# A hybrid encoder step on one core: the order planner is given longer instruction times

## The chip, the cores and the metric

The kernel runs on one core of one Trainium2 chip. The metric is device microseconds (us) of one execution; lower is better.

## The reference

One inference step of a streaming encoder layer (depth 1, width 1024) for 2048 prompt tokens with 16 learned meta tokens in front, and for 64 tokens of a running stream with 512 cached keys. Of each stream:

```
hn   = rms_norm(x, norm_mix_g)
proj = hn @ w_in                       # columns split among three head groups
o    = concat[ diff_attention(...),    # 4 heads, two softmaxes each, p0 - lam * p1, block-causal by chunks of 64
               rg_lru(...),            # causal conv of 4, gates, linear recurrence over the tokens
               gla(...) ]              # gated linear attention, 4 heads, blocks of 64
x    = x + o @ w_out
hn   = rms_norm(x, norm_ffn_g)
x    = x + (gelu(causal_dwconv3(hn @ w_up)) * (hn @ w_gate)) @ w_down
y    = rms_norm(x, norm_final_g)
```

Outputs are y of both streams, the new keys and values, and the final states of the recurrences and the convolutions.

## The kernel before

**Precision and tiles.** All 2128 tokens lie side by side as columns. Each factor of a large product is split into a high part and a rest, and each product is three passes on TensorE (high by high, high by rest, rest by high), in a `k` loop over 8 slices of 128 rows. `w_split` loads a weight tile `raw` in its first use, splits it into `whi` (ScalarE) and `wlo` (Pool or VectorE), and parks both in DRAM (`WS`), from where later uses reload them.

**Three streams.** `dense()` first runs `win()` (the combined projection, six token blocks, PSUM tile `ps_w`, L645 and L647), then `ffn_group(g)` for three groups of tokens (512; 512; 336 + 256 + 512): `wout` (L1437), `up_gate` (tiles `pu` and `pg`, L1302) and `down` (tile `pd`, L1369, added into `x` by VectorE at L1375). `attention()` runs over 9 token chunks by 4 heads. A unit's scores (L1056, L1063 into `ps_sc`, of which there are two buffers) are followed by a minimum on VectorE (L1065, `NB`), an exponential on ScalarE (L1066, `pc`) and, when a row's factors `fr` are known, a mix on Pool and VectorE (L157, L1104); then come transposes (L1155, `ps_pt`), their split on ScalarE and VectorE (`ph`, `pl`) and the product with V (L1170, `ps_o`). The last step of a unit is `oo`, stored to `OT`. `recurrent()` runs the RG-LRU and the GLA chunk by chunk (products L726, L895 and others into `ps_r`; a chain of VectorE, ScalarE and Pool steps such as L890 and L899 between them).

**Who sets the order.** `Flow.run` interleaves the three streams in program order by rough step costs written into the kernel. While attention issues, its priority number is lowered by 30000, and while the recurrences issue by 16000, so that these go ahead of dense work wherever they can. The orders on the engines are fixed at build time by a planner, which is switched on where the program is built:

```
    with tile.TileContext(nc, schedule_with_timeline_sim=True) as tc:
        tile_hymba_step(tc, *args)
```

It plays the program through with an assumed duration for each instruction. Each engine takes, of the instructions whose inputs and buffers are free at that moment of the play, the one with the lowest priority number. The orders of this play are final: on the chip each engine goes through its list and waits in front of any instruction whose inputs are late, with everything behind it on that engine waiting too. The same holds for SyncE, which issues nearly all transfers.

**Borders.** Group 1 of the FFN (tokens 512 to 1024) needs attention and recurrences of chunks 0 to 4; the last group needs all of them, since it reads `OT` and takes over their memory (`mstack.close()`, then `open3()`).

## Time and profile before

| | |
|---|---|
| median of 3 runs | 2975.56 us (2971.42 to 2979.68) |
| profiled execution, its own time | 2973.88 us |
| its span | 2972.1 us, 44691 instructions |
| TensorE busy | 2845.5 us, 96% |
| VectorE, ScalarE, Pool busy | 1868.5, 1084.9 and 765.9 us (63%, 37%, 26%) |
| mean granted TensorE clock | 0.98 of full |

The span is the stretch from the first to the last instruction of the profiled execution; 1.8 us of its time lie around it. A share of busy time is a mean over stages with different loads; the stages are told apart by windows below. Full speed of the granted clock is 2.4 GHz, and the lower level is 1.2 GHz.

### The profile page before, as it was taken

To read this page: it belongs to the slowest core of one execution; us is meant where nothing else is said; L and a number is where in the kernel's file an instruction comes from. 1 tells how busy PE (TensorE), PEld (TensorE's weight loads), DVE (VectorE), ACT (ScalarE), POOL (GpSimd) and SP (SyncE) were. 2 spreads that over 40 slices of the span, in tenths; PEclk is the share of its full clock that TensorE was granted. 3 is DMA by queue.
4 is the path that set the end of the run, shared out by engine and by line. 5 is a ranking of instruction groups with operands and counts; after the bars stand their busy time and mean duration, and the time that the engine had idled before them with its cause. 6 is when DMAs were issued, how large, how long until landed. Compare 5 with 4: busy or idle time off the path is not lost.

```text
span 2972.1 us, 44691 instructions
## 1 busy us (share of the span) xinstructions
PE 2845.5 (96%) x16031; PEld 2504.7 (84%) x16031; DVE 1868.5 (63%) x3757; ACT 1084.9 (37%) x2526; POOL 765.9 (26%) x1171
## 2 busy tenths in 40 slices
PE   6999999999999999999999999999999999999998
PEld 5988999999877777877777888888989999989997
DVE  6467674658688899899888764444454333333335
ACT  5354533454455554555553432112231121212122
POOL 4224231323244454445433210000120000000001
PEclk9999999999999999999999999999999999999998
DMA  9987776687995887878775655955222222222222
GB/s 327 325 282 208 244 245 217 218 265 227 286 332 185 283 252 241 273 251 265 242 263 180 216 186 194 336 196 189 82 86 86 86 86 86 86 86 86 85 85 105
DMA packets 293628, 592.31 MB, mean 199 GB/s; under 512 B 32758, under 2 KB 171774, under 8 KB 293406
## 3 DMA queue, kind: packets, MB, share of 16 engines
q1 hardware_dynamic: 293262, 589.44, 59.7%
q8 instruction: 127, 2.08, 0.3%
q14 instruction: 95, 0.78, 0.1%
q10 hardware_dynamic: 144, 0.01, 0.0%
HBM read 414.40 MB, written 174.96 MB: 198 GB/s over the span
## 4 chain that ended last, share of the span: by engine, by line
PE 50%; DVE 8%; DMA 2%; issue 1%; POOL 1%; ACT 1%; SPq 0%; POOLq 0%; ACTq 0%; DVEq 0%
PE pd L1369 15%; PE pu L1302 14%; PE pg L1302 13%; PE pd L1437 4%; DVE pc L1104 2%; PE ps_o L1170 1%; DVE NB L1065 1%; PE ps_pt L1155 1%; DVE BD L890 1%; PE ps_sc L1063 1%; DVE y L439 1%; PE ps_sc L1056 1%; DVE cc L1326 0%; DVE x L1375 0%; DVE pl L160 0%
## 5 line engine op out<-in xcount | busy, mean ns | idle before, releaser
L1326 DVE SCALAR_TENSOR_TENSOR cc<-uh,prm,cc 128x512 f32<-128x512 f32 (+4 forms) x264 | 164.0, 628 | 268.2 <-ACT cc L1324 264.8
L1066 ACT ACTIVATE pc<-ps_sc,NB 128x512 f32<-128x512 f32 (+6 forms) x400 | 224.7, 563 | 287.0 <-DVE NB L1065 243.4
L1375 DVE TENSOR_TENSOR x<-x,pd 128x512 f32<-128x512 f32 (+2 forms) x320 | 195.7, 617 | 199.4 <-PE pd L1369 198.3
L1302 PE MATMUL pu<-h2h,whi 128*128 128x512 f32 (+2 forms) x880 | 315.7, 359 | 3.1 <-ACT h2h L154 2.6
L1369 PE MATMUL pd<-gh,whi 128*128 128x512 f32 (+2 forms) x880 | 314.9, 359 | 3.9 <-DVE x L1375 2.3
L1302 PE MATMUL pg<-h2h,whi 128*128 128x512 f32 (+2 forms) x880 | 315.7, 359 | 2.0 <-DMA whi<-WS 2.0
L1302 PE MATMUL pu<-h2l,whi 128*128 128x512 f32 (+2 forms) x880 | 315.4, 359 | 0.4 <-DVE h2l L160 0.4
L1302 PE MATMUL pu<-h2h,wlo 128*128 128x512 f32 (+2 forms) x880 | 315.7, 359 | 0.0
L1302 PE MATMUL pg<-h2h,wlo 128*128 128x512 f32 (+2 forms) x880 | 315.7, 359 | 0.0
L1302 PE MATMUL pg<-h2l,whi 128*128 128x512 f32 (+2 forms) x880 | 314.5, 357 | 0.0
L1369 PE MATMUL pd<-gh,wlo 128*128 128x512 f32 (+2 forms) x880 | 312.9, 356 | 0.0
L1369 PE MATMUL pd<-gl,whi 128*128 128x512 f32 (+2 forms) x880 | 312.7, 356 | 0.0
L1319 ACT ACTIVATE uh<-pu 128x336 f32<-128x336 f32 (+3 forms) x132 | 59.3, 465 | 587.7 <-PE pu L1302 585.8
L645 PE MATMUL ps_w<-hh,whi 128*128 128x384 f32 (+2 forms) x768 | 260.2, 341 | 14.2 <-ACT whi L154 10.5
L645 PE MATMUL ps_w<-hh,wlo 128*128 128x384 f32 (+2 forms) x768 | 259.7, 338 | 12.0 <-DVE wlo L160 5.0
L1065 DVE TENSOR_REDUCE NB<-ps_sc 128x1 f32<-128x512 f32 (+6 forms) x400 | 209.5, 530 | 96.1 <-PE ps_sc L1063 94.5
L645 PE MATMUL ps_w<-hl,whi 128*128 128x384 f32 (+2 forms) x768 | 258.3, 337 | 0.1
L261 POOL TENSOR_TENSOR wlo<-raw,whi 128x1024 fp32r<-128x1024 f32 (+2 forms) x63 | 153.4, 2434 | 165.2 <-ACT whi L154 145.8
L157 POOL TENSOR_SCALAR gh<-cc 128x336 fp32r<-128x336 f32 (+3 forms) x132 | 69.6, 530 | 477.2 <-DVE cc L1339 375.6
L157 POOL TENSOR_SCALAR pc<-pc,fr 128x512 f32<-128x512 f32 (+4 forms) x200 | 167.1, 855 | 97.8 <-DVE fr L1086 88.9
L1369 PEld LDWEIGHTS pd<-gh,whi 128*128 128x128 f32 x880 | 165.7, 188 | 26.9 <-DVE x L1375 4.0
L1302 PEld LDWEIGHTS pu<-h2h,whi 128*128 128x128 f32 x880 | 167.0, 190 | 24.8 <-ACT h2h L154 2.8
(331 smaller groups left out, 6981.2 us busy)
## 6 DMA issues: line engine op xcount, KB each, us to landing
whi<-WS SPq DMA_DIRECT2D x202, 512.0 KB, 4.4
wlo<-WS SPq DMA_DIRECT2D x202, 512.0 KB, 5.0
WS<-whi SPq DMA_DIRECT2D x94, 512.0 KB, 4.3
WS<-wlo SPq DMA_DIRECT2D x94, 512.0 KB, 6.4
Kc<-KHL SPq DMA_DIRECT2D x48, 512.0 KB, 5.4
V<-VHL SPq DMA_DIRECT2D x48, 512.0 KB, 5.0
Q<-QHL SPq DMA_DIRECT2D x64, 256.0 KB, 5.1
raw<-in_wu SPq DMA_DIRECT2D x22, 512.0 KB, 4.2
```

Source lines behind the costliest of these rows:

```text
L157: nc.gpsimd.tensor_scalar(out, in_, s, 1.0, ALU.mult, ALU.mult)
L261: nc.gpsimd.tensor_tensor(out=lo[:, :n], in0=t[:, :n], in1=f(hi[:, :n]), op=ALU.subtract)
L645: nc.tensor.matmul(ps[:, :n], lhsT=wx, rhs=hx, start=st_, stop=sp_)
L1065: nc.vector.tensor_reduce(NB[:qw, ti, m, ci:ci + 1], ps[:qw, :kt_], AX.X, ALU.min)
L1066: nc.scalar.activation(out=pv_[m][:qw, :kt_], in_=ps[:qw, :kt_], func=AF.Exp, scale=-1.0, bias=NB[:qw, ti, m, ci:ci + 1], accum_out=SS[:qw ...
L1104: nc.vector.scalar_tensor_tensor(out=p0, in0=p0, scalar=u.R[:qw, ti, 0, ci:ci + 1], in1=p1, op0=ALU.mult, op1=ALU.add)
L1302: nc.tensor.matmul(ps[:, :n], lhsT=w_[wi_][:, k * P:(k + 1) * P], rhs=hx, start=(k == 0 and i3 == 0), stop=(k == KT - 1 and i3 == 2))
L1319: nc.scalar.activation(out=uh[:, 2:2 + m], in_=pu[:, a:b], func=AF.Copy)
L1326: nc.vector.scalar_tensor_tensor(out=cc[:, :m], in0=uh[:, w:w + m], scalar=cw[w], in1=cc[:, :m], op0=ALU.mult, op1=ALU.add)
L1369: nc.tensor.matmul(ps[:, :n], lhsT=w_, rhs=g_[:, o:o + n], start=(j == 0 and i3 == 0), stop=(j == len(gts) - 1 and i3 == 2))
L1375: nc.vector.tensor_tensor(x2[b, ct], x2[b, ct], ps[:, :n], ALU.add)
L1437: nc.tensor.matmul(ps[:, :n], lhsT=w_, rhs=g_, start=(k == 0 and i3 == 0), stop=(k == KT - 1 and i3 == 2))
```

## The change

Only the planner's assumptions are changed, at the head of the file, before anything is built. No instruction is added, removed or altered. The table `CYCLE_T` holds the planner's cycle time of each engine's data path: VectorE's is multiplied by 1.4, ScalarE's by 1.15 and Pool's by 1.2. `PE_FULL_CLOCK_PASS_GAP_NS` is the time that the planner puts behind each matmul at the full clock, over the streaming of its columns; it is set to 13 ns. Times of transfers, of semaphores and of weight loads stay as they are.

```diff
 import concourse.tile as tile
 from concourse import mybir
 from concourse._compat import with_exitstack
+from concourse.hw_specs import TRN2Spec
 from concourse.masks import make_identity
+
+
+TRN2Spec.CYCLE_T = {
+    mybir.EngineType.DVE: 1.4 * TRN2Spec.CYCLE_T[mybir.EngineType.DVE],
+    mybir.EngineType.Activation: 1.15 * TRN2Spec.CYCLE_T[mybir.EngineType.Activation],
+    mybir.EngineType.Pool: 1.2 * TRN2Spec.CYCLE_T[mybir.EngineType.Pool],
+}
+TRN2Spec.PE_FULL_CLOCK_PASS_GAP_NS = 13.0
```

## Rows read from the trace of the kernel before

**Rows 1.** The windows view, whole engines; columns: window, length, busy (instructions), PEclk, DMA share, GB/s.
```profile
0.00:1800.00 1800.00, 1693.24 (x9559) 1477.93 (x9560) 1381.27 (x2900) 848.74 (x2101) 654.93 (x876) 0.97 0.77 250
...
0.00:50.00 50.00, 33.24 (x168) 30.03 (x168) 34.41 (x84) 24.56 (x49) 21.76 (x32) 0.93 0.91 322
50.00:100.00 50.00, 36.74 (x202) 34.90 (x203) 23.75 (x40) 22.06 (x40) 23.40 (x17) 0.86 0.97 334
...
1800.00:2000.00 200.00, 200.00 (x903) 165.82 (x902) 87.39 (x129) 35.74 (x56) 15.72 (x54) 1.00 0.70 249
2400.00:2700.00 300.00, 300.00 (x1797) 273.58 (x1796) 110.70 (x202) 55.59 (x102) 21.84 (x77) 1.00 0.24 85
```

**Rows 2.** Windows of 50 us with the lowest granted clock.
```profile
200.00:250.00 50.00, 42.43 (x256) 38.14 (x255) 37.98 (x107) 20.90 (x72) 17.44 (x33) 0.90 0.80 253
800.00:850.00 50.00, 40.81 (x206) 31.91 (x205) 42.66 (x84) 29.90 (x73) 22.82 (x28) 0.83 1.00 327
900.00:950.00 50.00, 45.37 (x211) 37.06 (x210) 46.63 (x92) 22.32 (x54) 21.63 (x22) 0.90 0.54 165
1600.00:1650.00 50.00, 44.56 (x197) 34.89 (x196) 47.50 (x101) 23.14 (x57) 23.53 (x26) 0.86 0.40 128
```

**Rows 3.** Waits of TensorE, whole run: total us, times, longest us.
```profile
PE ps_sc L1056 <- ACT pc L1066: 15.5, 16, 2.6
PE ps_sc L1056 <- DMA Q<-QHL: 7.9, 6, 1.9
PE ps_r L895 <- DVE att L899: 5.3, 6, 2.0
PE ps_o L1170 <- DVE pl L160: 4.7, 5, 1.6
PE ps_w L645 <- DMA wlo<-WS: 3.9, 2, 2.9
```

**Rows 4.** TensorE's timeline behind one such wait: start us, us, engine, line, instruction.
```profile
1010.09 0.50 PE L1056 MATMUL ps_sc<-Kc,Q 128*128 128x512 f32 x1 [2.25 <-ACT pc L1066]
...
1012.89 0.63 PE L1369 MATMUL pd<-gh,whi 128*128 128x512 f32 x1
1013.32 0.63 PE L1369 MATMUL pd<-gh,wlo 128*128 128x512 f32 x1
```

**Rows 5.** The chain that ended last, two dense products: start us, us, passes.
```profile
1877.63 5.44 PE pu L1302 x24
...
2455.67 5.60 PE pu L1302 x24
```

**Rows 6.** Groups by line and shape, VectorE and ScalarE: busy us, mean ns, idle before.
```profile
L1065 DVE TENSOR_REDUCE NB<-ps_sc 128x1 f32<-128x512 f32 x192 | 130.0, 682 | 32.4 <-PE ps_sc L1063 32.0
L1104 DVE SCALAR_TENSOR_TENSOR pc<-pc,fr 128x512 f32<-128x512 f32 x96 | 100.4, 1076 | 4.7 <-POOL pc L157 4.7
L1065 DVE TENSOR_REDUCE NB<-ps_sc 128x1 f32<-128x384 f32 x64 | 35.0, 552 | 15.9 <-PE ps_sc L1063 15.7
L1330 DVE SCALAR_TENSOR_TENSOR uh<-uh,cc 128x512 f32<-128x512 f32 x44 | 30.4, 691 | 28.1 <-ACT uh L1329 28.1
L1066 ACT ACTIVATE pc<-ps_sc,NB 128x512 f32<-128x512 f32 x192 | 131.8, 687 | 178.8 <-DVE NB L1065 162.9 <-DVE pc L1104 8.2 <-PE ps_pt L1155 3.0
L1066 ACT ACTIVATE pc<-ps_sc,NB 128x384 f32<-128x384 f32 x64 | 37.1, 580 | 49.5 <-DVE NB L1065 31.2 <-PE ps_pt L1155 17.8
```

**Rows 7.** VectorE's timeline, work queued back to back: start us, us, instruction.
```profile
1060.60 0.68 DVE L1375 TENSOR_TENSOR x<-x,pd 128x512 f32<-128x512 f32 x1
1061.19 0.61 DVE L1337 SCALAR_TENSOR_TENSOR cc<-cc,pg 128x448 f32<-128x448 f32 x1
...
1067.43 0.17 DVE L1082 TENSOR_TENSOR SS<-SS,fr 128x16 f32<-128x16 f32 x1
...
1075.89 2.08 DVE L1086 TENSOR_TENSOR fr<-fr,st 128x16 f32<-128x16 f32 x1
```

**Rows 8.** Windows of VectorE alone: window, length, busy (instructions), PEclk, DMA share, GB/s.
```profile
900.00:1100.00 200.00, 181.27 (x344) 0.97 0.74 240
1100.00:1300.00 200.00, 181.93 (x341) 1.00 0.79 256
1300.00:1500.00 200.00, 180.92 (x364) 1.00 0.80 262
1500.00:1700.00 200.00, 160.67 (x324) 0.94 0.60 204
1700.00:1800.00 100.00, 63.69 (x110) 1.00 0.57 195
```

**Rows 9.** Attention's last `oo` on ScalarE; TensorE's first pass of the last group.
```profile
1846.46 0.42 ACT L154 ACTIVATE oo<-oSs 128x256 fp32r<-128x256 f32 x1 [2.09 <-DVE oSs L1196]
...
2036.59 0.32 PE L1437 MATMUL pd<-h2h,whi 128*128 128x336 f32 x1
```

## The prediction

> **What bounds the kernel now.** I read first the windows over the whole run [rows 1]. TensorE is busy 1693.24 of the first 1800 us and without a gap afterwards in the windows shown, so it sets the pace: from 1800 us on the dense products run back to back and no order can gain there. What an order can change lies before. Of the 106.8 us that TensorE idles up to 1800 us, 16.8 and 13.3 fall into the first two windows of 50 us, where the first weights are loaded and split; 76.7 are left between 100 and 1800 us, where attention and the recurrences are mixed into dense work.
>
> Next the waits [rows 3]. They are short, mostly 0.5 to 2.5 us, and they come from ScalarE and VectorE steps of attention (scores waiting for the exponential that frees their PSUM bank, 15.5 us in 16 waits, 0.97 us each) and of the recurrences, and some from transfers. The reader should see that in none of them is TensorE out of work: behind the waiting score matmul at 1010 us stand dense passes of L1369 whose inputs had long been there [rows 4]. The planner put the score first since in its play the exponential was done by then. That is a stall of order, not of capacity.
>
> The third view is the granted clock. A stall costs more than its idle time: after the 2.25 us at 1010 us the passes start 0.43 us apart [rows 4], which for 512 columns is one column per cycle at 1.2 GHz (426.7 ns), against 0.227 us in undisturbed work (24 passes in 5.44 us, [rows 5]). The four worst windows of 50 us [rows 2] have clocks of 0.90, 0.83, 0.90 and 0.86, which is 25.5 us of full clock missing; the mean of 0.97 up to 1800 us [rows 1], less the 10.5 us of the first 100, makes 43.5. I take the middle, 34 us, since part of the low clock falls on idle time anyway.
>
> Last VectorE: up to 1500 us it is over 90% busy for 600 us (181.27, 181.93 and 180.92 of 200, [rows 8]), so it is where lateness gathers.
>
> **The change, part by part.** No instruction changes, so each edit costs nothing by itself; what it does goes through the orders.
>
> The matmul's 13 ns: undisturbed passes of 512 columns take 226.7 ns [rows 5], 13.4 ns over 512 columns at 2.4 GHz (213.3); in the last group 233.3 (20 ns over), and 166.9 ns on average there [rows 1]. So 13 ns is what the trace shows for group 1, and still short for the last group. With a smaller gap the planner's TensorE runs ahead of the chip's, which by itself would give the other engines more time, not less; but it also makes VectorE's list expect a product before it exists. With this edit alone, dense work is stretched in the play, and more attention steps fit beside each product; for TensorE's waits it is a small loss or nothing, and I count nothing, as no row separates it. The Trainium skill ("TensorE: Matmul & The Clock Gate", section "Wait — 56ns, not 53.3ns?") gives about 2.5 ns over the columns per matmul; by that figure 13 would be too long by 10.5 ns a pass, and the trace, with 13.4 ns, disagrees.
>
> VectorE by 1.4: the minimum over scores takes 682 ns at 512 columns and 552 at 384 [rows 6], so 1.016 ns an element; 40% more on the 520 ns of streaming is 208 ns, and at most 273 if the fixed part is scaled too. ScalarE by 1.15: the exponential has 687 and 580 ns [rows 6], 0.836 ns an element, so 64 to 103 ns more. One link of score, minimum, exponential is therefore planned 0.27 to 0.38 us longer, and the next score matmul stands that much later in TensorE's list, with dense passes in front of it. Against a mean wait of 0.97 us that is 28 to 39% of a stall with one link; with the two links that a pair of PSUM buffers allows 56 to 78%. Pool by 1.2 acts through the mix and some GLA steps; its waits are a few us, and I count it with the rest.
>
> Is the longer time nearer the truth? The chip's VectorE runs alike work at very different times: three-operand steps of 512 columns take 691 ns at L1330 and 1076 at L1104 [rows 6], and a step on 16 columns takes 0.17 us or 2.08 [rows 7]. So part of lateness comes in bursts of about 2 us, which no factor on a cycle time foresees. The Trainium skill ("SBUF — State Buffer", section "Who interferes with whom") says that VectorE with two SBUF inputs and a GpSimd instruction that reads SBUF lock each other out for a whole instruction, and that issue order decides who waits. By that rule a uniform factor leaves the burst stalls where they are, which is the rival of no change below; the trace agrees that such bursts occur.
>
> The sum: of the 76.7 us idle, the two transfer rows (7.9 and 3.9, [rows 3]) are not touched by the edit, as the planner's transfer times stay; 65 are left. I take 45%, between one link and two, since queues lengthen the lead but bursts eat it: 29 us. Of the clock's 34 us the same share: 15. Against it I set 12 us of new waits, as much again as the transfer waits, because loads are issued from SyncE's fixed list and land at other places of the new order; that cost could be 0, or double. Net 29 + 15 - 12 = 32 us. The profiled execution's 2973.88 (span 2972.1 and 1.8 around it) becomes 2941.9; the median of the runs shown is 1.7 higher, so 2944. The cost is bounded below by a gain of all 99 us (2877), and above by the slow rival.
>
> **The rivals.**
>
> *No measurable change.* The bursts and the transfers decide, and the new order has as many stalls at other places; or the planner doesn't read the altered table at all and the program stays the same (I give that 0.03). For it: the longest waits are near 2 us, far above the 0.3 us that a link gains. Against it: the mean wait is 1 us, and over 90% load lets planned slack add up from step to step. Time 2975.
>
> *A gain twice as large.* Lead adds up along VectorE's queue, as its list is planned with 40% more time than work back to back needs (0.59 us between starts of steps of 512 columns, [rows 7], which would be planned as some 0.83). At 78% of 99 us and no give-back: 77 us, 2898.
>
> *Slower: VectorE becomes the bound of the play.* From 900 to 1800 us VectorE is busy 768 us [rows 8]; records overlap, and starts stand 0.59 us apart for records of 0.68 [rows 7], so the queue holds about 666 us of work. Times 1.4 that is 933 us in 900, and by the records 1076. In the first case the play just holds it, in the second attention and the recurrences end some 175 us later. Attention's last `oo` is at 1846.46 and the last group's first pass at 2036.59 [rows 9], a cover of 190 us. This rival decides when the stretch passes that: then the last attention units stand in TensorE's list behind all other work, and their chain, not TensorE, sets the pace. It also puts dense evacuations (L1375) behind attention's steps in VectorE's list, so that the three PSUM buffers of dense work stay full. If 190 us are passed by 40, half of it idle on the chip because its VectorE is faster than planned, and dense evacuations cost a 1 us wait in some 15 places, that is 20 + 15 = 35 us: 3010. For it: 91% load times 1.4. Against it: the cover of 190 us, and that TensorE's own plan gets longer by the 13 ns, which widens the cover.
>
> **How the numbers follow.** About 0.3% (9 us) is what a measurement of this kernel can tell from no change. Gain of about 32 us (2915 to 2966): 0.50. Gain of the larger kind, below 2915: 0.10. Within 2967 to 2984: 0.18. Slower: 0.22, of which half lies below 2992. So faster 0.60, same 0.18, slower 0.22. The likeliest case's own range is 2915 to 2966; the range for 8 in 10 leaves out some 0.09 below 2912 and 0.11 above 2992.
>
> **What the profile after would show.** If right: idle of TensorE between 100 and 1800 us falls from 76.7 to about 50, the wait of scores on ScalarE from 15.5 to about 8, fewer windows with a clock under 0.95; VectorE's load from 900 to 1500 falls below 90% as attention spreads out, and its last `oo` moves later than 1846 but stays before the last group. Busy time per instruction stays the same. Wrong would be: the same count of short waits at other lines (the rival of bursts), a larger sum of waits on transfers (my 12 us too small), or attention's end past the last group's start with TensorE idle near 2000 us (the slow rival). An order equal to the one before in every engine would show that the table was not read.

## The result: slower by half a per cent

The changed kernel takes 2988.68 us (median of 6 runs, 2982.20 to 2992.69) against 2972.85 us before (6 runs); the ratio is 1.0054, with a 95% interval of 1.0033 to 1.0074. The prediction was 2944 us, faster, in a range up to 2992: the time lies in the range, the sign is wrong.

The page of the profiled execution after the change; the second line has the busy time of each engine:

```profile
span 2990.5 us, 44661 instructions
...
PE 2860.8 (96%) x16031; PEld 2516.9 (84%) x16031; DVE 1849.2 (62%) x3757; ACT 1079.5 (36%) x2526; POOL 761.3 (25%) x1171
```

The working instructions are as many as before on every engine; the 30 fewer in the first line are all semaphore instructions. The same 16031 matmuls keep TensorE busy 15.3 us longer than before (2845.5), and it idles 129.7 us (2990.5 less 2860.8) instead of 126.6. So of the 18.4 us that the span grew, 3 are idle time and 15 are slower matmuls, which means a lower clock.

A profile is one execution, and the mean granted clock differs between executions of one kernel. In 69 executions of the kernel before it lies between 0.975 and 0.983 with a mean of 0.979, in the six of the changed kernel between 0.974 and 0.978 with a mean of 0.976. The profile above is the longest of these six (2992.69 us, clock 0.974). By the means, the clock takes some 9 us of the 15.8 by which the medians differ: 0.003 of 2980. Differences of clock between two profiles are to be read with that scatter, which is 24 us for the kernel before (0.008 of 2970).

The windows view after the change, whole engines, in the order PE, PEld, DVE, ACT, POOL, then granted clock, DMA share and GB/s; the first row answers to that of [rows 1], the others are the four with the lowest clock behind the first 100 us, as in [rows 2]:

```profile
0.00:1800.00 1800.00, 1692.83 (x9425) 1479.40 (x9426) 1324.80 (x2795) 826.50 (x2045) 629.60 (x853) 0.96 0.76 250
...
200.00:250.00 50.00, 42.56 (x229) 39.62 (x230) 34.23 (x82) 24.45 (x75) 11.98 (x21) 0.80 0.78 242
750.00:800.00 50.00, 41.22 (x267) 36.71 (x266) 34.85 (x66) 24.40 (x60) 12.21 (x16) 0.89 0.97 319
800.00:850.00 50.00, 45.26 (x195) 35.89 (x196) 37.28 (x87) 20.65 (x53) 17.48 (x32) 0.77 0.81 273
1450.00:1500.00 50.00, 43.13 (x196) 34.50 (x196) 40.05 (x72) 23.77 (x57) 16.29 (x20) 0.86 0.73 255
```

Summed over the windows of 50 us between 100 and 1900 us, the clock that is missing (50 us times one minus the clock) rose from 36.5 to 59.5 us.

TensorE's waits after the change, the longest sums (us, times, longest), answer to [rows 3]:

```profile
PE ps_sc L1065 <- DMA Q<-QHL: 18.9, 13, 3.1
PE ps_w L654 <- ACT whi L163: 16.6, 6, 6.9
PE ps_sc L1065 <- ACT pc L1075: 16.0, 19, 3.7
...
PE pg L1311 <- DMA whi<-WS: 5.0, 4, 2.8
PE ps_r L904 <- DVE att L908: 3.8, 1, 3.8
PE ps_w L654 <- DMA wlo<-WS: 3.5, 4, 1.1
PE ps_w L654 <- DMA whi<-WS: 3.3, 3, 1.5
```

Adding all rows of this view by what was waited for: engines (VectorE, ScalarE, Pool) 80.9 us, before 97.7; transfers 33.5 us, before 16.6; "issue", where the profile shows nothing that was waited for, 6.8 us, before 2.6. Between 100 and 1800 us, the stretch of the prediction, engines fell from 57.8 to 46.6 us, transfers rose from 14.6 to 27.8 and the number of waits went from 79 to 82. The reader should see that the change took away waits on engines, which it was built for, and that as much came back as waits on transfers. The largest of these is a unit's score matmul waiting for its queries `Q`.

One of them in the timeline of the changed kernel (SyncE's queue is SPq; start us, us):

```profile
1582.05 0.31 PE L1072 MATMUL ps_sc<-Kc,Q 128*128 128x144 f32 x1
...
1582.39 1.24 SPq L157 DMA_DIRECT2D Q<-QHL  x2
...
1587.46 0.77 PE L1065 MATMUL ps_sc<-Kc,Q 128*128 128x512 f32 x1 [2.39 <-DMA Q<-QHL]
...
1588.03 0.63 PE L1072 MATMUL ps_sc<-Kc,Q 128*128 128x512 f32 x1
...
1590.16 0.63 PE L1311 MATMUL pu<-h2l,whi 128*128 128x512 f32 x1
...
1591.10 0.39 PE L1311 MATMUL pu<-h2l,whi 128*128 128x512 f32 x1
```

`Q` has one buffer (`bufs=1`), so the next unit's queries are issued only when the last score of the unit before has read the old ones, at 1582 us. Such a load lands 5.1 us after its issue in the median, in both traces, which show the landing of 24 and 12 of these loads. The next score stands so early in TensorE's list that 2.39 us of the landing are not covered, and the matmuls behind it run at the low clock (records of 0.63 us, as in [rows 4]) until 1591 us, where the records are 0.39 us again.

Of the signs that the prediction gave for being right, three did not come: TensorE's idle time between 100 and 1800 us rose from 76.7 to 81.9 us, scores still wait 16.0 us for ScalarE, and eight windows of 50 us between 100 and 1900 us have a clock under 0.95, before five. The others came: VectorE is busy 87% between 900 and 1500 us (523.91 of 600), attention's last `oo` is at 1957.5 us, 111 us later than in [rows 9], and the last group's first pass is at 2052.3.

### The profile page after: what moved, and what is told of

Its sections match the earlier page's. It is cut to its first block, busy times and chain, and to the rows that moved or that the text cites. A ratio compares the mean times of both kernels' runs of the same rounds, so it can differ in the third digit from the quotient of the medians.

```text
span 2990.5 us, 44661 instructions
## 1 busy us (share of the span) xinstructions
PE 2860.8 (96%) x16031; PEld 2516.9 (84%) x16031; DVE 1849.2 (62%) x3757; ACT 1079.5 (36%) x2526; POOL 761.3 (25%) x1171
## 4 chain that ended last, share of the span: by engine, by line
PE 79%; DMA 10%; DVE 5%; ACT 2%; POOL 2%; issue 1%; SPq 1%; POOLq 0%; ACTq 0%; DVEq 0%
PE pu L1311 16%; PE pd L1378 15%; PE pg L1311 15%; PE ps_w L654 9%; PE pd L1446 6%; PE ps_o L1179 4%; PE ps_w L656 3%; DMA Q<-QHL 2%; PE ps_sc L1072 2%; PE ps_sc L1065 2%; PE ps_pt L1164 2%; PE ps_r L904 2%; DMA wlo<-WS 1%; DVE pc L1113 1%; DMA raw<-in_wi 1%
## 5 line engine op out<-in xcount | busy, mean ns | idle before, releaser
L1378 PE MATMUL pd<-gh,whi 128*128 128x512 f32 (+2 forms) x880 | 321.3, 367 | 4.5 <-DVE x L1384 3.1
L654 PE MATMUL ps_w<-hh,whi 128*128 128x384 f32 (+2 forms) x768 | 261.0, 342 | 20.5 <-ACT whi L163 16.6
L1328 ACT ACTIVATE uh<-pu 128x336 f32<-128x336 f32 (+3 forms) x132 | 59.5, 464 | 548.8 <-PE pu L1311 542.3
L1065 PE MATMUL ps_sc<-Kc,Q 128*128 128x512 f32 (+6 forms) x400 | 152.6, 382 | 41.2 <-DMA Q<-QHL 18.9
L1311 PEld LDWEIGHTS pg<-h2h,whi 128*128 128x128 f32 x880 | 166.2, 189 | 29.1 <-issue 4.5
L1378 PEld LDWEIGHTS pd<-gh,whi 128*128 128x128 f32 x880 | 167.2, 190 | 27.8 <-DVE x L1384 4.4
```

The lines of the kernel that those rows point to most:

```text
L654: nc.tensor.matmul(ps[:, :n], lhsT=wx, rhs=hx, start=st_, stop=sp_)
L1065: nc.tensor.matmul(ps[:qw, :kt_], lhsT=Q[:, 0, m, qo:qo + qw], rhs=Kc[:, m, :kt_], start=True, stop=False)
L1311: nc.tensor.matmul(ps[:, :n], lhsT=w_[wi_][:, k * P:(k + 1) * P], rhs=hx, start=(k == 0 and i3 == 0), stop=(k == KT - 1 and i3 == 2))
L1378: nc.tensor.matmul(ps[:, :n], lhsT=w_, rhs=g_[:, o:o + n], start=(j == 0 and i3 == 0), stop=(j == len(gts) - 1 and i3 == 2))
```

## The experiments

Three theories stood after the result. A: orders are slow when TensorE's list has matmuls in front of transfers that the plan lands too early; lengthening engine times and not transfers makes that likelier. B: every small change of the plan draws another order, and the times scatter for no reason that can be named. C: VectorE's 1.4 alone costs the time, by pushing attention late. Medians of 4 to 12 runs and ratios to the kernel before on the same chip follow (for the changed kernel, of the runs above); the last two columns are sums of rows of TensorE's waits, and of the windows of 50 us between 100 and 1900 us, each from one profiled execution.

| kernel | us | ratio, 95% interval | waits on transfers; on engines | clock missing |
|---|---|---|---|---|
| before | 2969 to 2973 | 1 | 16.6; 97.7 | 36.5 |
| changed | 2988.7 | 1.0054 [1.0033, 1.0074] | 33.5; 80.9 | 59.5 |
| gap_only | 3001.9 | 1.0098 [1.0083, 1.0113] | 31.1; 99.2 | 58.5 |
| dve_only | 2992.7 | 1.0076 [1.0058, 1.0093] | 28.0; 94.4 | 49 |
| act_pool_only | 2964.7 | 0.9985 [0.9974, 0.9996] | 13.4; 100.5 | 34 |
| dve_139 | 2989.0 | 1.0059 [1.0042, 1.0077] | 41.3; 83.6 | 45.5 |
| dve_101 | 2959.9 | 0.9970 [0.9960, 0.9980] | 12.0; 95.9 | 29 |
| gap_3 | 3001.5 | 1.0104 [1.0091, 1.0117] | 25.8; 106.7 | 52.5 |
| late_after | 2970.4 | 1.0004 [0.9994, 1.0015] | 14.2; 92.5 | 47.5 |
| late_before | 2961.0 | 0.9970 [0.9958, 0.9982] | 7.3; 101.3 | 38.5 |
| late_gap_3 | 2957.1 | 0.9955 [0.9940, 0.9970] | 6.7; 99.8 | 37 |
| late_gap_13 | 2972.6 | 1.0005 [0.9992, 1.0018] | 7.7; 110.2 | 38.5 |
| late_dve | 2978.3 | 1.0026 [1.0014, 1.0037] | 21.3; 86.5 | 59 |
| late3_before | 2942.2 | 0.9907 [0.9891, 0.9924] | 0.9; 94.6 | 29 |
| late3_after | 2940.0 | 0.9908 [0.9894, 0.9922] | 11.3; 77.4 | 31.5 |
| late3_gap_3 | 2956.8 | 0.9953 [0.9940, 0.9965] | 1.1; 97.4 | 44 |
| late3_dve_101 | 2959.3 | 0.9966 [0.9954, 0.9978] | 1.6; 108.8 | 35 |
| late45_before | 2958.8 | 0.9965 [0.9953, 0.9978] | 0.3; 106.2 | 31.5 |

**Parts of the change.** gap_only (against the changed kernel, as all edits up to dve_139):

```diff
-    mybir.EngineType.DVE: 1.4 * TRN2Spec.CYCLE_T[mybir.EngineType.DVE],
+    mybir.EngineType.DVE: 1.0 * TRN2Spec.CYCLE_T[mybir.EngineType.DVE],
-    mybir.EngineType.Activation: 1.15 * TRN2Spec.CYCLE_T[mybir.EngineType.Activation],
+    mybir.EngineType.Activation: 1.0 * TRN2Spec.CYCLE_T[mybir.EngineType.Activation],
-    mybir.EngineType.Pool: 1.2 * TRN2Spec.CYCLE_T[mybir.EngineType.Pool],
+    mybir.EngineType.Pool: 1.0 * TRN2Spec.CYCLE_T[mybir.EngineType.Pool],
```

> Only the matmul's 13 ns is given to the planner; the cycle times stay. Theory A (the engine times grow in the plan while the transfers' times don't, so that score matmuls stand in front of loads that have not landed): no engine time but TensorE's is changed, and its 5% is near the truth, so about the time of before, 2973 us, waits of scores on Q near the 7.9 us of before. Theory B (any change of the plan's times draws another order, and orders differ by some 10 us for no reason that can be named): anywhere in 2960 to 2990. Theory C (VectorE's 1.4 alone pushes attention late and costs the time): 2973 us, with attention's last score near 1763 us.

It is the slowest kernel of all, 32 us over the one before. Such a loss doesn't need what theory C names: VectorE's times are untouched and attention's last score is at 1765 us, 2 us from where it was before. Theory A, too, expected no loss here.

dve_only:

```diff
-    mybir.EngineType.Activation: 1.15 * TRN2Spec.CYCLE_T[mybir.EngineType.Activation],
+    mybir.EngineType.Activation: 1.0 * TRN2Spec.CYCLE_T[mybir.EngineType.Activation],
-    mybir.EngineType.Pool: 1.2 * TRN2Spec.CYCLE_T[mybir.EngineType.Pool],
+    mybir.EngineType.Pool: 1.0 * TRN2Spec.CYCLE_T[mybir.EngineType.Pool],
-TRN2Spec.PE_FULL_CLOCK_PASS_GAP_NS = 13.0
```

> Only VectorE's cycle time is 1.4 times as long in the plan. Theory A: most of the loss, 2982 to 2989 us, and waits of scores on Q of 14 to 19 us. Theory B: anywhere in 2960 to 2990, waits on Q not tied to the time. Theory C: the whole loss, about 2989 us, with attention's last score near the 1865 us of the changed kernel.

Slower by 0.76%, with 14.0 us of waits on Q; attention's last score is at 1879 us, so that by itself this kernel fits theory C as well as A. Two parts that cost 32 and 23 us alone cost 16 together with the third: the parts don't add.

act_pool_only:

```diff
-    mybir.EngineType.DVE: 1.4 * TRN2Spec.CYCLE_T[mybir.EngineType.DVE],
+    mybir.EngineType.DVE: 1.0 * TRN2Spec.CYCLE_T[mybir.EngineType.DVE],
-TRN2Spec.PE_FULL_CLOCK_PASS_GAP_NS = 13.0
```

> Only ScalarE's 1.15 and Pool's 1.2. Theory A: a small part of the loss, 2976 to 2980 us, waits on Q of 9 to 12 us. Theory B: anywhere in 2960 to 2990. Theory C: 2973 us.

Faster by 0.15%, waits on Q 7.7 us as before. Theory A expected a small loss here.

**Neighbours.** dve_139:

```diff
-    mybir.EngineType.DVE: 1.4 * TRN2Spec.CYCLE_T[mybir.EngineType.DVE],
+    mybir.EngineType.DVE: 1.39 * TRN2Spec.CYCLE_T[mybir.EngineType.DVE],
```

> The changed kernel with 1.39 in place of 1.4 for VectorE, a difference too small to mean anything for any wait. Theories A and C: the time of the changed kernel, 2989 us within 3 us, and the same waits on Q (18.9 us within 3). Theory B: a time that differs from 2989 by 5 to 15 us either way, and other waits.

The time of the changed kernel within 0.4 us, and 21.2 us of waits on Q, within the 3 forecast. That speaks for A, but the mix is another: 41.3 us of waits on transfers in all, not 33.5, and 45.5 of missing clock, not 59.5. Nor does it hold at other places, as the next two show.

dve_101 (the kernel before with this alone):

```diff
+TRN2Spec.CYCLE_T = {
+    **TRN2Spec.CYCLE_T,
+    mybir.EngineType.DVE: 1.01 * TRN2Spec.CYCLE_T[mybir.EngineType.DVE],
+}
```

> The kernel before with VectorE's cycle time 1% longer in the plan and nothing else: too little to mean anything for a wait, though the orders differ from those of before. Theory A (relative times of engines and transfers): 2970 us within 3 and waits of scores on Q near 8 us. Theory B (an order is a draw, and the order before was a good one): slower by 5 to 25 us, with waits on Q anywhere between 8 and 20.

Faster by 0.3%, by 1% of planned time, with 5.5 us of waits on Q. Neither theory had that: A expected no change, B a loss.

gap_3 (the kernel before with this alone):

```diff
+TRN2Spec.PE_FULL_CLOCK_PASS_GAP_NS = 3.6
```

> The kernel before with the matmul's gap about 1 ns longer in the plan, at 3.6 ns. Theory A: a tenth of the loss of 30 us that 13 ns alone gave, so 2973 us. Theory B: a draw, 2960 to 3000, and not a tenth of the way to the kernel with 13 ns.

A nanosecond costs as much as ten did. So the size of the loss says nothing of the size of the change, and theory B holds for which order one gets. What the slow orders share is in the table: the five kernels with 25 us or more of waits on transfers are the five that take 2988 us or more, and those with fewer than 17 all take less than 2973. Within the five the order is not that of the waits: dve_139 has the most and is one of the two fastest.

**Transfers planned later.** The planner's delay between the issue of a transfer on SyncE and its start is lengthened; nothing on the chip changes but the orders. late_after is the changed kernel with this, late_before the kernel before:

```diff
+TRN2Spec.DGE_DMA_DELAY = {
+    **TRN2Spec.DGE_DMA_DELAY,
+    mybir.EngineType.SP: TRN2Spec.DGE_DMA_DELAY[mybir.EngineType.SP] + 1500,
+}
```

> The changed kernel, and the planner is told that every transfer issued by SyncE starts 1.5 us later. Theory A: scores no longer stand in front of loads that have not landed; waits on Q fall from 18.9 to under 8 us and the time to 2965 to 2976. Theory B: a draw, 2965 to 3000; the waits on Q may fall, and other waits take their place.

> The kernel before, and the planner is told that every transfer issued by SyncE starts 1.5 us later. Theory A: a small gain, 2960 to 2968, with waits on Q under 4 us. Theory B: a draw, 2965 to 3000.

Waits on Q fall to 3.9 and 0.5 us, both times are within A's bounds, and the changed kernel loses its loss (1.0004). The next three put the same edit on the other slow orders: late_gap_3 is the kernel before with the edit above and this:

```diff
+TRN2Spec.PE_FULL_CLOCK_PASS_GAP_NS = 3.6
```

late_gap_13 has 13.0 there, and late_dve has in its place VectorE's factor of 1.4, written as that of dve_101. (gap_only and dve_only write a table of the three engines alone, these two keep the planner's other entries, if it has any.)

> The kernel with the matmul's gap at 3.6 ns (3001.5 us, waits on transfers 25.8 us in all), and transfers planned 1.5 us later. Theory A (what is lost in the slow orders is TensorE standing in front of transfers that the plan lands too early): waits on transfers under 17 us and 2957 to 2973 us. Theory B (each order is a draw, and the two kernels with late transfers were good draws): 2960 to 3000, with even odds of more than 2980.

> The kernel with the matmul's 13 ns alone (3001.9 us, waits on transfers 31.1 us), and transfers planned 1.5 us later. Theory A: waits on transfers under 17 us, 2957 to 2973 us. Theory B: 2960 to 3000.

> The kernel with VectorE's 1.4 alone (2992.7 us, waits on transfers 28 us), and transfers planned 1.5 us later. Theory A: waits on transfers under 17 us, 2957 to 2973 us. Theory B: 2960 to 3000.

All three are faster than without it, by 44, 29 and 14 us. late_dve misses A's bounds: 2978 us, with 21.3 us of waits on transfers, 14.1 of them on Q, as before the edit; why 1.5 us did nothing for Q there was not tried. The waits of scores on ScalarE and on Q in gap_3:

```profile
PE ps_sc L1061 <- ACT pc L1071: 22.7, 24, 3.1
...
PE ps_sc L1061 <- DMA Q<-QHL: 12.8, 9, 2.7
...
PE pd L1442 <- DMA whi<-WS: 4.5, 1, 4.5
```

and in late_gap_3:

```profile
PE ps_sc L1065 <- ACT pc L1075: 21.5, 20, 2.6
...
PE ps_sc L1065 <- DMA Q<-QHL: 6.0, 3, 3.3
...
PE ps_w L654 <- DMA whi<-WS: 0.5, 1, 0.5
```

The wait on ScalarE stays, those on transfers go or are halved. In all, between these two profiles the waits on transfers fall by 19.1 us, those on engines by 6.9 and the missing clock by 15.5, together 41.5 of the 43.3 us that the span fell (2999.2 to 2955.9).

late3_before has 3000 in place of 1500:

> The kernel before, transfers planned 3 us later. Theory A: waits on scores' Q stay under 2 us and the time between 2955 and 2968; more lead than the transfers need gains nothing over 1.5 us. Theory B: a draw, 2960 to 3000.

2942 us, 0.93% faster than before, better than A expected. Of the waits on transfers 0.9 us is left:

```profile
PE ps_w L653 <- DMA wlo<-WS: 0.7, 2, 0.4
...
PE pg L1310 <- DMA whi<-WS: 0.2, 1, 0.2
```

Whether that was a lead that transfers need or one lucky draw, and whether the change has a price of its own, was asked of four more. late3_after is the changed kernel, late3_gap_3 and late3_dve_101 are gap_3 and dve_101, each with 3000; late45_before is the kernel before with 4500.

> The changed kernel, transfers planned 3 us later. Theory A: waits on transfers under 5 us; with these out of the way the change itself is neither gain nor loss, so within 10 us of the kernel before with 3 us (2942). Theory D (the change's longer VectorE time has a price of its own, since it packs late work behind later work): 2955 to 2975, with waits on transfers as low.

> The matmul's gap at 3.6 ns, transfers planned 3 us later. Theory A: 2935 to 2955 and waits on transfers under 5 us. Theory B (draws): 2940 to 2990.

> VectorE 1% longer, transfers planned 3 us later: another order next to that of 2942 us, for the spread of draws where transfers are planned late. Theory A: 2935 to 2955, waits on transfers under 5 us. Theory B: 2940 to 2990.

> The kernel before, transfers planned 4.5 us later. Theory A: nothing left to gain by waits on transfers (0.9 us with 3 us), 2938 to 2955. Theory B: 2940 to 2990.

The changed kernel with 3 us takes 2940 us, like the kernel before with 3 us, and not theory D's 2955 to 2975: a price of the change's own is not seen once transfers are planned late, though one smaller than the scatter of these orders could hide in it. Its waits on engines are the lowest of all (77.4 us); 11.3 us of waits on transfers are left, over A's 5. It also tells against theory C: its last score is at 1802 us, 38 later than in the kernel before (1763), and it is 30 us faster. The neighbours come out at 2957 and 2959 us, outside of A's 2935 to 2955 though their waits on transfers are gone (1.1 and 1.6 us); so is 4.5 us with 2959. That is theory B's part: with transfers out of the way the orders still scatter by some 19 us, now from 2940 to 2959. Both kernels at 2940 are the fastest measured; they beat the kernel before and the changed one.

If planning transfers later only drew other orders, slow orders would get faster by it and fast ones slower. All orders together speak against that: the eight without it take 2960 to 3002 us, the five with 1.5 us 2957 to 2978, the five with 3 or 4.5 us 2940 to 2959. Waits on transfers go the same way (12.0 to 41.3 us, 6.7 to 21.3, 0.3 to 11.3), and those on engines don't (80.9 to 106.7, 86.5 to 110.2, 77.4 to 108.8).

## Why the prediction was wrong

**What bounds the kernel** held. Short waits of TensorE before 1800 us, and the low clock near them, are what the experiments took away or added.

**The engine times** held in direction and were too large in size. Forecast were 29 us between 100 and 1800 us; the waits on engines fell by 11.2 there (57.8 to 46.6) and by 16.8 in the whole run (97.7 to 80.9). The mechanism is seen in all kernels with VectorE's 1.4 or 1.39: their six sums lie between 77.4 and 94.4, those of the eleven other experiments and of the kernel before between 94.6 and 110.2. The wait that I had named, scores on ScalarE, didn't fall (15.5 to 16.0, forecast 8). And of the 65 us of which the share was taken only 57.8 were waits on engines.

**The new waits**, 12 us, were 16.9 (16.6 to 33.5), within the bounds that I had given. I had put them down to transfers that land at other places. In the wait on `Q` shown above the load was issued as soon as its buffer was free, and it is TensorE that reaches the matmul too early. I read `Q`'s 7.9 us in [rows 3] as something that the edit doesn't touch, and set it aside, while it was the largest wait on a transfer and grew to 18.9.

**The step that failed is "Of the clock's 34 us the same share: 15".** Instead of giving back 15 us the clock took more: in the profiles TensorE's busy time for the same matmuls grew by 15.3 us and the missing clock by 23 (36.5 to 59.5), and by the means of all executions the loss is some 9 us. That is 24 to 38 us off, more than the other two terms together. Idle time, +3.1, and busy time, +15.3, make up the 18.4 us that the span grew; forecast was -29 + 12 - 15.

I had let the clock follow the idle time that the engine waits leave. That failed twice. Idle time as a whole didn't fall, since what engines gave back transfers took. And the waits on engines that went were not those at the low clock: between 100 and 1900 us, in windows of 50 us with a clock of 0.95 or more they fell from 35 to 22 us, in those with a lower clock they rose from 23 to 25, and waits on transfers there rose from 6 to 15 (each wait counted in the window in which it ends). One of these windows after, 900 to 950 us with a clock of 0.92:

```profile
PE ps_o L1179 <- ACT ph L163: 3.8, 2, 3.0
PE ps_sc L1065 <- DMA Q<-QHL: 3.1, 1, 3.1
PE ps_sc L1065 <- ACT pc L1075: 0.3, 1, 0.3
```

That the waits on transfers bring the lower clock is not shown. In gap_3 and its late twin both fall (by 19.1 and 15.5), and in the changed kernel with 3 us too (by 22.2 and 28), but in late_dve the waits fell by 6.7 and the missing clock rose by 10. The mean clock of all executions says the same: it rises from 0.973 to 0.980 from gap_3 to late_gap_3 and from 0.974 to 0.980 from gap_only to late_gap_13, but it stays at 0.976 from the changed kernel to late_after, which is 18 us faster all the same, and falls from 0.977 to 0.974 from dve_only to late_dve. So what sets the larger part of the loss, the clock, stays open.

**The matmul's 13 ns**, which I counted at nothing, costs 32 us alone. The forecast had no row to separate it, and took that for no effect. A nanosecond does the same (gap_3), so it is not its size that counts but which order it draws.

**The slow rival** had the sign but not the mechanism. VectorE's load fell to 87%, attention's end kept 95 us of cover before the last group (1957.5 to 2052.3), and between 1800 and 2050 us TensorE idled under 2 us. The rival of no change was nearest in mechanism, as many stalls at other places (79 waits became 82), but I gave it no loss. The Trainium skill ("SBUF — State Buffer", section "Who interferes with whom") says that a VectorE instruction with two SBUF inputs contends with a GpSimd (Pool) instruction that reads SBUF. No run here tells how much of the engine waits left comes from such bursts, which that rival named.

**Open** is why a nanosecond or 40% on VectorE draws an order with early matmuls and 1% on VectorE does not, and what makes two orders without waits on transfers differ by 17 us (late3_before and late3_dve_101). Part of the latter is 14 us more of waits on engines and 6 of clock; what sets them was not tried. Open is also, as said, what sets the clock.

## What to carry to other kernels

When a planner fixes the orders, look in the trace for the waits of the bound engine on transfers and compare the landing time with the distance between issue and first use in its list: here one buffer and 5.1 us made the largest of these waits, and giving the planner 3 us more for transfers was worth 0.9 to 1.5% in three orders (before, changed, gap_3) and nothing in a fourth (dve_101), where 10.4 us of waits on transfers went and 12.9 us of waits on engines came. Scaling engine times without transfers can shift that balance, and so can any other edit of the plan. A single changed order is a draw: before its time is put down to a reason, run neighbours that mean nothing (1% here, a nanosecond there); in this kernel they moved the time by -0.3% and +1.0%. And a clock read from one profile is one execution's: compare it over several.

## What the runs showed of the hardware that was not expected

A stall costs more than its idle time, and how much more differs between orders. With the same 16031 matmuls, TensorE's idle and busy time are 104.8 and 2835.1 us in late3_before. In the changed kernel there are 25 us more of idle time (129.7) and 26 more of busy time (2860.8); in gap_only 38 more of idle time (142.5) and 20 of busy time (2854.8); in late_dve 15 (119.7) and 21 (2856.5). A straight line through all 18 profiles gives 0.4 us of busy time for each microsecond of idle time, with a wide scatter. The longer busy time goes with the granted clock: in the windows of 50 us between 100 and 1900 us late3_before misses 29 us of clock, and these three 59.5, 58.5 and 59.
